# Side work of two feed-forward networks in another order, stores and copies issued by other engines, and a residual added one group later

## The chip, the cores and the metric

The kernel runs on one core of a Trainium2 chip, in one launch. The metric is the time in microseconds (us) of one execution on the device. Engines are named as in the profile: PE multiplies matrices (PEld loads its weights), DVE, ACT and POOL work on tiles, SP issues DMA transfers; sixteen DMA engines move the data.

## The reference, cut to what matters

One layer of a hybrid decoder for 1024 prompt tokens and 64 sample tokens (8 sequences of 8), with a model width of 1024:

```python
x = x + 0.5 * swiglu(rmsnorm(x, ffn1_norm), ffn1_w_gu, ffn1_w_down)
h = rmsnorm(x, mix_norm)
z = h @ w_in                                   # q, k, v, LRU inputs, memory queries, three gates
y_att = attend(q, k, v, rel_bias)              # dilated windows; new window caches are outputs
xc, conv_new = causal_conv(xr, conv_buf, conv_w, conv_b)
y_rec = gelu(yr) * rglru(xc, ...)
y_mem = memory_attention(qm, mk, mv)
merged = sum over branches of sigmoid(gate + b) * (y @ w_o)
x = x + merged @ w_out
x = x + 0.5 * swiglu(rmsnorm(x, ffn2_norm), ffn2_w_gu, ffn2_w_down)
y = rmsnorm(x, final_norm)
# swiglu(h, w_gu, w_down) = (silu(h @ gate) * (h @ up)) @ w_down, hidden width 2816
```

Each output window cache of the sample tokens is the old cache shifted by the 8 new rows, so most of it is a copy from memory to memory.

## The kernel before

All large products run as three matmuls with a high and a low part of both operands (`mac3`, L262 to L264). A weight tile `wr` of 512 columns is split by ACT into its high part (`part`, L167) and by DVE into the low part `ws` (L168). The plan of weights is fixed, SP loads the tiles in its order (L154), and seven split parts (`RING`) may be ready ahead. The stages follow each other: FFN1 gate and up (to 556 us), its down projection (to 815), memory branch, gates and attention (to 1396), the recurrent branch, called LRU (to 1745), the merge of the branches, the output projection (to 2000), FFN2 gate and up (to 2505), its down projection (to 2785), the last norm.

*FFN gate and up.* The 1088 tokens are two halves (`tp`) of 544, each in two chunks of 272 (`TC`). The hidden width has 22 tiles of 128. Three of them are plain (`plain`), with operands `xo` of the raw x split in high and low part; meanwhile the norms are made (`norms_of_blocks`: ACT squares, POOL adds in L412), x is multiplied by the gain vector (`gain_blocks`, L426 on POOL or L430 on ACT) and sums and differences of blocks of x are made (`sums_of_blocks`, L438). The other tiles are quads: seven products of sums of blocks instead of eight, in the order of `OPS`, which is 1, 6, 7, 5, 2, 4, 3. Their weights are sums and differences of quarters a11, a12, a21, a22 of the gate and up weights (`combined`, L183 on DVE and POOL). `swiglu` empties the banks: DVE writes `uu` and `sl` (L539, L554), POOL multiplies by 1/rms (L557, L561); then `gated_hidden` has ACT apply silu (L503), POOL multiply `sl` by `uu` (L506) and SP store the tile to memory as `h_d` (L509), two, three and four steps later. The last two quads of each half run for that half alone. At the start of each tile, `copies` issues cache copies on SP (L1539); there are 42 of them.

*Down projection.* `h_d` is loaded again and split; groups of two hidden tiles add to x in SBUF (`down_tile`, L645), 24 tiles of output per group. In FFN2 the x to add to is loaded from memory by SP before (L1790).

*LRU.* `lru_tile` runs six times; between its steps PE works on chunks of the gates (tile `z`, emptied by DVE in L1383), two gates per tile. `att_combine` joins the attention groups for eight blocks of 128 tokens as a side job (DVE's weights `mw`, POOL's L871 and L873, PE's transpose in L832). `merge` loads the branch outputs as `ystage` (L1414), has ACT and DVE split them (L1420, L1421) and multiplies.

*Order.* Every engine runs its instructions in the order in which the program emits them. `tick()` is called once in every product (after four of its k steps); it runs the functions that `later(n, f)` put down for n ticks on and one step of the generators in `K.first` and `K.side`. So a number of steps says how many products later something is emitted, not when it runs. Each DMA waits for an earlier one on the same one of eight lanes. `norm_chunk` makes 1/rms of a chunk: matmul with ones (L294), DVE (L296, L298), POOL's power (L299), a matmul that spreads it over the partitions (L306), and DVE's copy `rbc` (L307). The last norm scales by `final` (L1516, L1518).

## Time and profile before

| | us |
|---|---|
| median of 3 runs (2795.2 to 2798.28) | 2796.01 |
| the profiled execution | 2796.95 |
| its span, first to last instruction | 2795.1 |
| PE busy in it | 2673.1 (96%) |
| DVE, ACT, POOL busy | 1718.9, 892.1, 808.4 |
| mean granted clock of PE | 0.981 |

Busy times are of one execution. PE is busy when any matmul is in it, at full or at half clock; a granted clock below 1 in a stretch means that part of it ran at the lower level. A bracket behind a timeline row is the idle time of that engine before the row and what ended it.

### The profile page before, as it was taken

To read this page: it belongs to the slowest core of one execution; us is meant where nothing else is said; L and a number is where in the kernel's file an instruction comes from. 1 tells how busy PE (TensorE), PEld (TensorE's weight loads), DVE (VectorE), ACT (ScalarE), POOL (GpSimd) and SP (SyncE) were. 2 spreads that over 40 slices of the span, in tenths; PEclk is the share of its full clock that TensorE was granted. 3 is DMA by queue.
4 is the path that set the end of the run, shared out by engine and by line. 5 is a ranking of instruction groups with operands and counts; after the bars stand their busy time and mean duration, and the time that the engine had idled before them with its cause. 6 is when DMAs were issued, how large, how long until landed. Compare 5 with 4: busy or idle time off the path is not lost.

```text
span 2795.1 us, 46229 instructions
## 1 busy us (share of the span) xinstructions
PE 2673.1 (96%) x18076; PEld 2588.7 (93%) x18076; DVE 1718.9 (61%) x3003; ACT 892.1 (32%) x1693; POOL 808.4 (29%) x734
## 2 busy tenths in 40 slices
PE   7789999999999999999989999999989999989997
PEld 7789999899999899989978889899989999979997
DVE  5545666767774433567687556763556666666766
ACT  6222232311144322323334354421623232231112
POOL 4445554400030000112144211231445454440003
PEclk9899999999999999999999999999999999999998
DMA  4223434522234252565555432854526432243221
GB/s 163 82 101 136 157 127 135 208 89 94 94 139 142 75 163 79 175 194 178 172 157 157 142 100 73 281 175 164 180 96 220 167 109 79 77 138 120 89 77 64
DMA packets 180570, 374.97 MB, mean 134 GB/s; under 512 B 21288, under 2 KB 115688, under 8 KB 179680
## 3 DMA queue, kind: packets, MB, share of 16 engines
q1 hardware_dynamic: 180352, 372.02, 40.1%
q8 instruction: 142, 2.33, 0.3%
q14 instruction: 76, 0.62, 0.1%
HBM read 305.59 MB, written 113.16 MB: 150 GB/s over the span
## 4 chain that ended last, share of the span: by engine, by line
PE 79%; DVE 6%; POOL 4%; issue 4%; DMA 4%; ACT 2%; SPq 0%; DVEq 0%; ACTq 0%; POOLq 0%
PE pg L262 9%; PE pg L264 9%; PE pg L263 9%; PE z L262 7%; PE z L264 7%; PE z L263 7%; PE pd L262 6%; PE pd L263 6%; PE pd L264 6%; DMA h_d<-sl 2%; PE po L264 2%; PE po L263 2%; PE po L262 2%; PE o L811 1%; PE wo L262 1%
## 5 line engine op out<-in xcount | busy, mean ns | idle before, releaser
L262 PE MATMUL pg<-xo,ws 128*128 128x272 f32 x2512 | 735.6, 293 | 51.1 <-ACT ws L167 27.6
L264 PE MATMUL pg<-xo,ws 128*128 128x272 f32 x2512 | 730.7, 291 | 5.5 <-DVE ws L168 5.5
L263 PE MATMUL pg<-xo,ws 128*128 128x272 f32 x2512 | 730.4, 291 | 0.0
L167 ACT ACTIVATE ws<-wr 128x512 fp32r<-128x512 f32 x592 | 349.6, 614 | 979.2 <-PE pd L264 385.3
L168 DVE TENSOR_TENSOR ws<-wr,ws 128x512 fp32r<-128x512 f32 x592 | 482.3, 837 | 183.6 <-ACT ws L167 182.2
L262 PEld LDWEIGHTS pg<-xo,ws 128*128 128x128 f32 x2512 | 480.4, 191 | 57.0 <-ACT ws L167 28.0
L264 PEld LDWEIGHTS pg<-xo,ws 128*128 128x128 f32 x2512 | 480.1, 191 | 6.3 <-DVE ws L168 6.3
L263 PEld LDWEIGHTS pg<-xo,ws 128*128 128x128 f32 x2512 | 480.7, 191 | 0.0
L262 PE MATMUL z<-xg,ws 128*128 128x368 f32 (+1 forms) x1392 | 476.2, 342 | 1.1 <-DVE ta L1383 1.1
L264 PE MATMUL z<-xg,ws 128*128 128x368 f32 (+1 forms) x1392 | 458.2, 329 | 0.0
L263 PE MATMUL z<-xg,ws 128*128 128x368 f32 (+1 forms) x1392 | 457.9, 329 | 0.0
L645 DVE TENSOR_TENSOR x<-x,pd 128x352 f32<-128x352 f32 (+1 forms) x528 | 270.9, 530 | 153.0 <-PE pd L264 147.1
L262 PE MATMUL pd<-h,ws 128*128 128x368 f32 (+1 forms) x1056 | 348.8, 330 | 8.0 <-DVE x L645 8.0
L263 PE MATMUL pd<-h,ws 128*128 128x368 f32 (+1 forms) x1056 | 347.6, 329 | 0.0
L264 PE MATMUL pd<-h,ws 128*128 128x368 f32 (+1 forms) x1056 | 346.4, 328 | 0.0
L262 PEld LDWEIGHTS z<-xg,ws 128*128 128x128 f32 x1392 | 263.3, 189 | 16.4 <-issue 13.5
L263 PEld LDWEIGHTS z<-xg,ws 128*128 128x128 f32 x1392 | 263.7, 189 | 1.1
L264 PEld LDWEIGHTS z<-xg,ws 128*128 128x128 f32 x1392 | 262.6, 189 | 0.0
L262 PEld LDWEIGHTS pd<-h,ws 128*128 128x128 f32 x1056 | 199.4, 189 | 8.6 <-DVE x L645 8.6
L264 PEld LDWEIGHTS pd<-h,ws 128*128 128x128 f32 x1056 | 200.0, 189 | 0.0
L263 PEld LDWEIGHTS pd<-h,ws 128*128 128x128 f32 x1056 | 199.6, 189 | 0.0
L557 POOL TENSOR_TENSOR uu<-uu,rbc 128x544 f32<-128x544 f32 x76 | 109.3, 1442 | 290.3 <-DVE uu L539 290.0
(290 smaller groups left out, 3578.0 us busy)
## 6 DMA issues: line engine op xcount, KB each, us to landing
wr<-in_w_gu_dram SPq DMA_DIRECT2D x96, 512.0 KB
wr<-in_w_in_dram SPq DMA_DIRECT2D x58, 512.0 KB
qb<-qs_d SPq DMA_DIRECT2D x48, 512.0 KB
h_d<-sl SPq DMA_DIRECT2D x88, 272.0 KB
hr<-h_d SPq DMA_DIRECT2D x44, 544.0 KB
wr<-in_w_dn_dram SPq DMA_DIRECT2D x44, 512.0 KB
out_sk_dram<-in_cache_k_dram SPq DMA_DIRECT2D x16, 1020.0 KB
out_sv_dram<-in_cache_v_dram SPq DMA_DIRECT2D x16, 1020.0 KB
```

The costliest lines, as they stand in the source:

```text
L167: nc.scalar.activation(spl[:, 0, :n], src, AF.Copy)
L168: nc.vector.tensor_tensor(out=spl[:, 1, :n], in0=src, in1=spl[:, 0, :n].bitcast(F32), op=OP.subtract)
L262: nc.tensor.matmul(out, wh, xh, start=start and i == 0, stop=False, **more)
L263: nc.tensor.matmul(out, wh, xl, start=False, stop=False, **more)
L264: nc.tensor.matmul(out, wl, xh, start=False, stop=i == n - 1, **more)
L557: nc.gpsimd.tensor_tensor(out=t["uu"], in0=t["uu"], in1=rb, op=OP.mult)
L645: nc.vector.tensor_tensor(out=xa, in0=xa, in1=ps[:, :n], op=OP.add)
L811: nc.tensor.matmul(po[:, e], pt[:, h, j * 128:(j + 1) * 128], z["vt"][:, kb[j], e], start=j == 0, stop=j == len(kb) - 1)
```

## The change

- `combined` makes the two sums of weights first (`s1` and `s2` have tiles of their own, a22 is kept), issues POOL's subtraction into a21 before the first part and that into a12 before the part of a22.
- In `norms_of_blocks` the engine that adds the squares is an argument: DVE for one half, POOL for the other; each square is added by itself.
- In the plain phase of both FFNs the gains of both halves are issued step by step beside each other, one on ACT and one on POOL, and the sums of both halves are DVE's.
- `gated_hidden` runs silu, product and store 4, 5 and 7 steps later in quads and 1, 2 and 3 in plain tiles. The store is issued by ACT; the cache copies are issued by POOL.
- `lru_constants` is spread over 20 steps.
- `att_combine` lets two more steps pass for blocks 2 and 3; the first two LRU tiles have one gate fewer, and the two gates left over run in `merge`, one third ahead of the loads, one third behind them and one third between the splits.
- In FFN2's down projection the first group's tiles are copied by ACT into x; during the second group SP loads x row by row and POOL adds it, eight steps later.
- `norm_chunk` spreads its result two steps later in FFN1's down projection, and runs later at the end; DVE adds every second square of the last chunk; the finals come three steps later.

```diff
-            mix += [col("w_in", 18 + r), col("w_in", 24 + r)] + take(FILL[2])
+            mix += [col("w_in", 18 + r), col("w_in", 24 + r)] + take(FILL[2] - (r < 2))
...
-        s2 = self.sums.tile([128, 544], F32, name=self.uid("s2"), tag="s2", bufs=2)[:, :512]
+        s1, s2 = (self.sums.tile([128, 512], F32, name=self.uid("s2"), tag="s2", bufs=2) for _ in range(2))
...
+        tt(nc.vector, s1, a21, a22, OP.add)
+        tt(nc.vector, s2, s1, a11, OP.subtract)
+        tt(nc.gpsimd, a21, a11, a21, OP.subtract)
         put(1, a11)
         yield
-        put(4, a22)
-        tt(nc.vector, a22, a21, a22, OP.add)
-        tt(nc.vector, s2, a22, a11, OP.subtract)
-        tt(nc.gpsimd, a21, a11, a21, OP.subtract)
-        yield
         put(6, s2)
         yield
         put(7, a21)
         yield
-        put(5, a22)
+        put(5, s1)
         yield
         put(2, a12)
         tt(nc.gpsimd, a12, a12, s2, OP.subtract)
+        yield
+        put(4, a22)
         yield
         put(3, a12)
         yield
...
-    def norms_of_blocks(self, tp, xs, pool):
+    def norms_of_blocks(self, tp, xs, pool, eng):
...
+                for k in range(4):
                     if i or k:
-                        for e in range(2):
-                            nc.gpsimd.tensor_tensor(out=acc, in0=acc, in1=t[:, e], op=OP.add)
+                        t = self.sums.tile([128, 512], F32, name=self.uid("sq"), tag="s2", bufs=2)[:, :TC]
                     else:
-                        nc.gpsimd.tensor_tensor(out=acc, in0=t[:, 0], in1=t[:, 1], op=OP.add)
+                        t = acc
+                    nc.scalar.activation(t, self.block(xs, i, j)[:, k], AF.Square)
+                    if i or k:
+                        eng.tensor_tensor(out=acc, in0=acc, in1=t, op=OP.add)
...
-                        self.gated_hidden(p, tp, sl, uu)
+                        self.gated_hidden(p, tp, sl, uu, (1, 2, 3))
...
-    def gated_hidden(self, p, tp, sl, uu):
+    def gated_hidden(self, p, tp, sl, uu, steps=(4, 5, 7)):
...
-            nc.sync.dma_start(self.h_d[p, :, tp * TH:(tp + 1) * TH], sl.rearrange("p j n -> p (j n)"))
+            nc.scalar.dma_start(self.h_d[p, :, tp * TH:(tp + 1) * TH], sl.rearrange("p j n -> p (j n)"))
...
-        for n, f in ((2, silu), (3, mult), (4, store)):
+        for n, f in zip(steps, (silu, mult, store)):
...
-                        self.down_tile([wd(j, (o - o0) * 128) for j in range(nk)], ks, o, c)
+                        self.down_tile([wd(j, (o - o0) * 128) for j in range(nk)], ks, o, c, residual and g == 0)
+                    if residual and g == 1:
+                        residual(o)
...
-    def down_tile(self, ws, ks, o, c):
+    def down_tile(self, ws, ks, o, c, new=False):
         nc = self.nc
         t0, n = CH[c]
         ps = self.mm_bank("pd")
         self.mac3(ps[:, :n], [(w, tuple(self.h[k][:, s, t0:t0 + n] for s in range(2))) for w, k in zip(ws, ks)])
         xa = self.x[:, o, t0:t0 + n]
-        nc.vector.tensor_tensor(out=xa, in0=xa, in1=ps[:, :n], op=OP.add)
+        if new:
+            nc.scalar.activation(xa, ps[:, :n], AF.Copy)
+        else:
+            nc.vector.tensor_tensor(out=xa, in0=xa, in1=ps[:, :n], op=OP.add)
         self.tick()
...
-            for _ in range(3):
+            for _ in range(5 if b in (2, 3) else 3):
...
-        nc.vector.tensor_tensor(out=e, in0=lam, in1=neg, op=OP.min)
-        nc.scalar.activation(e, e, AF.Exp)
...
+
+        def low():
...
+        for n, f in ((6, low), (10, lambda: nc.scalar.activation(e, e, AF.Exp)), (14, inverse), (20, series)):
+            self.later(n, f)
...
-    def merge(self, pool, gates):
+    def merge(self, pool, last):
...
-        gates()
+        wg = [self.unit("w_in", 128) for _ in last]
+
+        def gates(c):
+            for f, w in zip(last, wg):
+                ps = self.mm_bank("z")
+                self.mac3(ps[:, :CH[c][1]], [(w(k, 0), self.xgk(c, k)) for k in range(KD)])
+                if c == 2:
+                    self.done()
+                self.gate_evac(f, c, ps)
+                self.tick()
+        gates(0)
         stage = self.xgp.tile([128, 2 * KD, CMAX], F32, name="ystage", tag="xg")
...
             load(2, k, 3 * j)
+        gates(1)
         for j, k in enumerate(TRI):
+            if j == 2:
+                gates(2)
             split(2, k, 3 * j)
...
-            self.tc.keep_in_program_order(self.nc.sync.dma_start(d, s))
+            self.tc.keep_in_program_order(self.nc.gpsimd.dma_start(d, s))
...
-    norms = [K.norms_of_blocks(tp, xs[tp], ev) for tp in range(2)]
+    norms = [K.norms_of_blocks(tp, xs[tp], ev, eng) for tp, eng in enumerate((nc.vector, nc.gpsimd))]
...
-        yield from K.gain_blocks(xs[0], g, nc.scalar)
+        for _ in zip(K.gain_blocks(xs[0], g, nc.scalar), K.gain_blocks(xs[1], g, nc.gpsimd)):
+            yield
         yield from K.sums_of_blocks(0, xs[0], nc.vector)
         spare.close()
         late.append(right(spare, "late1"))
-        yield from K.gain_blocks(xs[1], g, nc.gpsimd)
-        yield from K.sums_of_blocks(1, xs[1], nc.gpsimd, lambda: K.plained)
...
-                K.later(6 if c < 2 else 2, lambda: K.norm_chunk(c, acc[c], 3 if c < 2 else 2))
+                K.later(6 if c < 2 else 2, lambda: K.norm_chunk(c, acc[c], 5 if c < 2 else 2))
...
-                gate(FILL[2])
+                gate(FILL[2] - (i < 2))
...
-        K.merge(pool, lambda: gate(24))
+        K.merge(pool, gates)
...
-        yield from K.norms_of_blocks(0, xs[0], ev)
-        yield from K.gain_blocks(xs[1], g, nc.scalar)
+        yield from K.norms_of_blocks(0, xs[0], ev, nc.vector)
+        for _ in zip(K.gain_blocks(xs[1], g, nc.scalar), K.gain_blocks(xs[0], g, nc.gpsimd)):
+            yield
         yield from K.sums_of_blocks(1, xs[1], nc.vector)
...
-        yield from K.gain_blocks(xs[0], g, nc.gpsimd)
-        yield from K.sums_of_blocks(0, xs[0], nc.gpsimd, lambda: K.plained)
+        yield from K.sums_of_blocks(0, xs[0], nc.vector, lambda: K.plained)
...
-        K.first += [K.operands_of_blocks(1, xs[1], g, order, store(1)), K.norms_of_blocks(1, xs[1], ev)]
+        K.first += [K.operands_of_blocks(1, xs[1], g, order, store(1)), K.norms_of_blocks(1, xs[1], ev, nc.gpsimd)]
...
-        for o in range(KD):
-            nc.sync.dma_start(K.x[:, o], K.x_d[1][:, o])
...
+        def residual(o):
+            t = pool.tile([128, NT], F32, name=K.uid("xr"), tag="xr", bufs=2)
+            nc.sync.dma_start(t, K.x_d[1][:, o])
+            K.later(8, lambda: nc.gpsimd.tensor_tensor(out=K.x[:, o], in0=K.x[:, o], in1=t, op=OP.add))
...
-                K.sumsq(o, xa, acc[c], n)
+                K.sumsq(o, xa, acc[c], n, nc.vector if c == 2 and o % 2 else None)
...
-                K.later(3, lambda: K.norm_chunk(c, acc[c], 2))
+                K.later(5, lambda: K.norm_chunk(c, acc[c], 3))
                 for j in range(4):
-                    K.later(6 + j, lambda j=j: K.final(c, 2 * j))
...
+                    K.later(9 + j, lambda j=j: K.final(c, 2 * j))
...
+        K.down("w_dn2", ring, K.raw_tiles(pool), after2, residual)
```

First place: the end of the plain tiles of FFN1. These are POOL's rows before (`xs_108` is the x of the second half, `rs` the 1/rms, `sl` the hidden tile, `wr` a weight tile):

```order
L506 TENSOR_TENSOR sl_173<-sl_173,uu_174 128x544
L506 TENSOR_TENSOR sl_347<-sl_347,uu_348 128x544
L426 TENSOR_TENSOR xs_108<-xs_108,vec 128x4x272 x2
L506 TENSOR_TENSOR sl_558<-sl_558,uu_559 128x544
L426 TENSOR_TENSOR xs_108<-xs_108,vec 128x4x272 x2
L438 TENSOR_TENSOR xs_108<-xs_108 128x4x272 x4
L183 TENSOR_TENSOR wr_624<-wr_588,wr_624 128x512
L506 TENSOR_TENSOR sl_720<-sl_720,uu_721 128x544
```

and POOL's rows now, from the second gain row's place on:

```order
L425 TENSOR_TENSOR xs_108<-xs_108,vec 128x4x272
L505 TENSOR_TENSOR sl_173<-sl_173,uu_174 128x544
L425 TENSOR_TENSOR xs_108<-xs_108,vec 128x4x272
L299 TENSOR_TENSOR rs_572<-rs_572,mhalf 128x4
L425 TENSOR_TENSOR xs_108<-xs_108,vec 128x4x272
L1563 DMA out_sv_dram<-in_cache_v_dram 8x2x15360
L425 TENSOR_TENSOR xs_108<-xs_108,vec 128x4x272
L505 TENSOR_TENSOR sl_361<-sl_361,uu_362 128x544
L505 TENSOR_TENSOR sl_590<-sl_590,uu_591 128x544
```

DVE's rows now at the same place (`xo` are split operands, `pg` the banks of the plain tiles, `xs_107` is the first half):

```order
L374 TENSOR_TENSOR xo_4_93_730<-xs_107,xo_4_93_730 128x1088
L475 TENSOR_TENSOR sl_590<-pg_687,rbc 128x272
L475 TENSOR_TENSOR uu_591<-pg_716,rbc 128x272
L437 TENSOR_TENSOR xs_108<-xs_108 128x4x272 x3
L374 TENSOR_TENSOR xo_6_97_771<-xs_108,xo_6_97_771 128x1088
L374 TENSOR_TENSOR xo_7_99_800<-xs_108,xo_7_99_800 128x1088
L437 TENSOR_TENSOR xs_108<-xs_108 128x4x272
```

POOL's sums of `xs_108` in L438 are gone from its queue and stand in DVE's as L437, behind the evacuations of a plain tile; the gains stand further ahead, and a cache copy stands between two of them.

Second place: a quad of FFN1. SP's rows before, with the two stores of a quad and the copy behind them:

```order
L154 DMA wr_2872<-in_w_gu_dram 128x1024
L509 DMA h_d<-sl_2737 128x544
L509 DMA h_d<-sl_2751 128x544
L1539 DMA out_sk_dram<-in_cache_k_dram 16x16320
L154 DMA wr_3107<-in_w_gu_dram 128x1024
L154 DMA wr_3109<-in_w_gu_dram 128x1024
```

ACT's rows now (silu is L502, the weight parts L167, the stores L508):

```order
L167 ACTIVATE ws_2423<-wr_2150 128x512
L502 ACTIVATE sl_2292<-sl_2292 128x544
L502 ACTIVATE sl_2306<-sl_2306 128x544
L167 ACTIVATE ws_2461<-s_2419 128x512
L508 DMA h_d<-sl_2292 128x544
L167 ACTIVATE ws_2496<-wr_2152 128x512
L508 DMA h_d<-sl_2306 128x544
L167 ACTIVATE ws_2527<-s_2418 128x512
L167 ACTIVATE ws_2558<-wr_2150 128x512
```

and POOL's rows now in a quad:

```order
L556 TENSOR_TENSOR uu_1238<-uu_1238,rbc 128x544
L560 TENSOR_TENSOR sl_1286<-sl_1286,rbc 128x272
L560 TENSOR_TENSOR sl_1300<-sl_1300,rbc 128x272
L1563 DMA out_sk_dram<-in_cache_k_dram 2x8x16128
L183 TENSOR_TENSOR wr_1190<-wr_1188,wr_1190 128x512
L505 TENSOR_TENSOR sl_1286<-sl_1286,uu_1223 128x544
L505 TENSOR_TENSOR sl_1300<-sl_1300,uu_1238 128x544
```

The stores stand between weight parts of the next quad, one part apart; the copy stands behind the two L560 rows and ahead of the first weight difference and the products.

Third place: PE at the start of the LRU stage, the transposes of block 2 of `att_combine` (`oc`) among z chunks, before:

```order
L262 MATMUL z_14257<-xg_7987,ws_13991 128x352
L263 MATMUL z_14257<-xg_7987,ws_13991 128x352
L264 MATMUL z_14257<-xg_7987,ws_13991 128x352
L832 MATMUL t_14299<-ident,oc_13893 128x128 x2
L262 MATMUL z_14328<-xg_8093,ws_13865 128x368
L263 MATMUL z_14328<-xg_8093,ws_13865 128x368
```

and now (L1333 is the first matmul of the second LRU tile, on the output `xc` of its convolution):

```order
L262 MATMUL z_14435<-xg_8257,ws_14040 128x368
L263 MATMUL z_14435<-xg_8257,ws_14040 128x368
L264 MATMUL z_14435<-xg_8257,ws_14040 128x368
L1333 MATMUL g_14468<-xc_14307,lw_13881 128x352
L1333 MATMUL g_14471<-xc_14307,lw_13881 128x352
L836 MATMUL t_14474<-ident,oc_13942 128x128 x2
L262 MATMUL z_14507<-xg_8036,ws_14043 128x352
```

The transposes have moved behind two more z chunks, and two matmuls that need the convolution of LRU tile 1 now stand right before them.

## Rows read from the trace of the kernel before

**Rows 1.** The head of the page (the span; busy time, share of the span and count of each engine), and the core's mean granted TensorE clock.

```profile
span 2795.1 us, 46229 instructions
...
PE 2673.1 (96%) x18076; PEld 2588.7 (93%) x18076; DVE 1718.9 (61%) x3003; ACT 892.1 (32%) x1693; POOL 808.4 (29%) x734
...
core 0: 2795.1 us, clock 0.981
```

**Rows 2.** What PE waited for over the whole span: PE's output and line <- engine, output and line waited for: us in total, times, longest.

```profile
PE pg L262 <- ACT ws L167: 27.6, 3, 11.6
...
PE pd L262 <- DVE x L645: 8.0, 2, 7.0
PE t L832 <- POOL oc L873: 7.5, 1, 7.5
...
PE t L1003 <- ACT yt L834: 5.3, 1, 5.3
```

**Rows 3.** Eleven stretches: start and end in us, width, then busy time (and instructions) of PE, of its weight loads, of DVE, ACT and POOL, the granted TensorE clock, the busy share of the DMA engines, GB/s.

```profile
8.00:50.00 42.00, 32.88 (x220) 31.46 (x220) 22.45 (x51) 27.85 (x56) 24.81 (x31) 0.92 0.47 184
79.90:95.20 15.30, 0.94 (x4) 0.56 (x3) 5.15 (x6) 4.33 (x6) 11.31 (x5) 0.61 0.19 78
160.00:280.00 120.00, 107.47 (x806) 104.70 (x805) 62.84 (x111) 31.47 (x57) 62.67 (x68) 0.96 0.34 122
515.00:557.00 42.00, 35.44 (x242) 34.00 (x240) 30.86 (x49) 17.75 (x30) 19.36 (x14) 0.92 0.75 280
804.00:815.00 11.00, 8.30 (x42) 7.99 (x41) 10.88 (x22) 8.11 (x18) 8.85 (x8) 0.84 0.42 152
1396.00:1459.00 63.00, 49.10 (x264) 46.76 (x263) 55.38 (x88) 24.05 (x32) 28.57 (x28) 0.92 0.56 174
1748.00:1763.00 15.00, 8.71 (x37) 7.28 (x36) 6.27 (x7) 6.10 (x9) 0.00 (x0) 0.76 0.99 337
2056.00:2072.00 16.00, 5.27 (x28) 4.74 (x27) 7.63 (x9) 4.36 (x7) 10.11 (x5) 0.72 0.39 130
2464.00:2487.00 23.00, 17.84 (x123) 16.73 (x122) 17.65 (x28) 10.13 (x18) 10.42 (x7) 0.91 0.27 93
2505.00:2514.00 9.00, 2.03 (x8) 1.73 (x7) 3.15 (x6) 0.00 (x0) 0.45 (x1) 0.78 0.68 246
2766.00:2786.00 20.00, 12.26 (x68) 10.85 (x66) 15.82 (x32) 9.66 (x18) 12.01 (x11) 0.84 0.40 148
```

**Rows 4.** Timeline at the end of the plain tiles of FFN1, in the order of engines DVE, POOL, ACT, PE: start, duration, engine and line, operation, tiles, count, and in brackets the idle time before and what ended it.

```profile
57.60 3.94 DVE L438 TENSOR_TENSOR xs<-xs 128x1088 f32<-128x1088 f32 x3
...
75.90 0.42 DVE L476 TENSOR_TENSOR uu<-pg,rbc 128x272 f32<-128x272 f32 x1
...
77.37 3.96 POOL L426 TENSOR_TENSOR xs<-xs,vec 128x1088 f32<-128x1088 f32 x2
81.29 10.16 POOL L438 TENSOR_TENSOR xs<-xs 128x1088 f32<-128x1088 f32 x4
...
88.91 2.11 ACT L373 ACTIVATE xo<-xs 128x1088 fp32r<-128x1088 f32 x2 [12.93 <-POOL xs L438]
...
91.59 0.59 PE L262 MATMUL pg<-xo,ws 128*128 128x272 f32 x1 [11.62 <-ACT ws L167]
```

**Rows 5.** Around a late store, timelines of SP's DMA issues, of DVE and of PE, one step of the chain of waits (the store, from issue to landing), what DVE waited for between 95 and 300 us, and one stretch with the columns of rows 3. The last two are an issue and a use of a sl buffer in a later, undisturbed quad.

```profile
126.00 0.64 SPq L1539 DMA_DIRECT2D out_sk_dram<-in_cache_k_dram  x1
...
143.39 24.00 DMA h_d<-sl
...
167.48 0.44 DVE L554 TENSOR_TENSOR sl<-pg,rbc 128x272 f32<-128x272 f32 x1 [15.46 <-DMA h_d<-sl]
...
167.97 0.39 PE L262 MATMUL pg<-xo,ws 128*128 128x272 f32 x1 [4.40 <-DVE sl L554]
...
DVE sl L554 <- DMA h_d<-sl: 35.3, 4, 15.5
...
163.00:167.50 4.50, 0.57 (x5) 0.35 (x3) 0.02 (x1) 0.00 (x0) 0.00 (x0) 1.00 0.12 47
...
353.72 2.11 SPq L509 DMA_DIRECT2D h_d<-sl  x2
...
364.62 0.44 DVE L554 TENSOR_TENSOR sl<-pg,rbc 128x272 f32<-128x272 f32 x1 [1.05 <-PE pg L264]
```

**Rows 6.** The stretch around the two waits at the start of the LRU stage, with the columns of rows 3.

```profile
1436.00:1460.00 24.00, 11.23 (x46) 10.65 (x45) 20.85 (x47) 5.13 (x10) 11.56 (x13) 0.76 0.58 179
```

**Rows 7.** Timeline: ACT in the merge, DVE at the start of the second down projection, DVE near the end.

```profile
1757.43 3.15 ACT L1420 ACTIVATE ys<-ystage 128x1104 fp32r<-128x1104 f32 x3 [4.37 <-DMA ystage<-y_d]
...
2511.85 3.34 DVE L645 TENSOR_TENSOR x<-x,pd 128x352 f32<-128x352 f32 x7 [5.85 <-DMA x<-x_d]
...
2780.14 2.39 DVE L1516 SCALAR_TENSOR_TENSOR x<-x,vec,rbc 128x368 f32<-128x368 f32 x4
```

**Rows 8.** Timeline rows of POOL in two quads one after the other, the stretch between them with the columns of rows 3, and a row of ACT in the last, single quads.

```profile
337.04 1.80 POOL L183 TENSOR_TENSOR wr<-wr,wr 128x512 f32<-128x512 f32 x1 [3.92 <-DVE wr L183]
...
357.81 1.80 POOL L183 TENSOR_TENSOR wr<-wr,wr 128x512 f32<-128x512 f32 x1 [2.33 <-DVE wr L183]
...
337.00:357.80 20.80, 20.80 (x169) 20.80 (x168) 13.12 (x22) 6.09 (x11) 10.81 (x8) 1.00 0.58 173
...
541.63 0.63 ACT L167 ACTIVATE ws<-wr 128x512 fp32r<-128x512 f32 x1 [5.31 <-POOL wr L183]
```

More of the change, by code (lines that the diff above doesn't have):

```diff
@@ L405, in norms_of_blocks @@
             for i in range(2):
-                for k in (0, 2):
-                    t = self.sums.tile([128, 544], F32, name=self.uid("sq"), tag="s2", bufs=2)
-                    t = t.rearrange("p (k n) -> p k n", k=2)
-                    nc.scalar.activation(t, self.block(xs, i, j)[:, k:k + 2], AF.Square)
+                for k in range(4):
                     if i or k:
-                        for e in range(2):
-                            nc.gpsimd.tensor_tensor(out=acc, in0=acc, in1=t[:, e], op=OP.add)
-                    else:
-                        nc.gpsimd.tensor_tensor(out=acc, in0=t[:, 0], in1=t[:, 1], op=OP.add)
+                        t = self.sums.tile([128, 512], F32, name=self.uid("sq"), tag="s2", bufs=2)[:, :TC]
+                    else:
+                        t = acc
+                    nc.scalar.activation(t, self.block(xs, i, j)[:, k], AF.Square)
+                    if i or k:
+                        eng.tensor_tensor(out=acc, in0=acc, in1=t, op=OP.add)
                 if i:
@@ L460, in plain @@
             xo = self.xo[tp]
-            sl, uu = (pool.tile([128, 2, TC], F32, name=self.uid(x), tag=x, bufs=3) for x in ("sl", "uu"))
+            sl, uu = (pool.tile([128, 2, TC], F32, name=self.uid(x), tag=x, bufs=n) for x, n in (("sl", 3), ("uu", 3)))
             for j, ms in enumerate(((1, 2), (0, 3))):
@@ L614, in gate_up, with down @@
             self.tick()
-    def down(self, dn, pool, raws, after):
+    def down(self, dn, pool, raws, after, residual=None):
         for g, (k, nk, w) in enumerate(DOWN):
@@ L1255, in lru_constants, with inverse, series @@
         nc.gpsimd.tensor_scalar(neg, lam, -1.0, None, op0=OP.mult)
[L1256 to L1270 removed]
+        def low():
+            nc.vector.tensor_tensor(out=e, in0=lam, in1=neg, op=OP.min)
+            nc.vector.tensor_scalar(neg, neg, 0.0, 4.0, op0=OP.max, op1=OP.mult)
+        def inverse():
+            nc.vector.tensor_scalar(z, e, 2.0, None, op0=OP.add)
+            nc.vector.reciprocal(z, z)
+        def series():
+            nc.gpsimd.tensor_tensor(out=z, in0=z, in1=e, op=OP.mult)
+            nc.gpsimd.tensor_tensor(out=z2, in0=z, in1=z, op=OP.mult)
+            nc.gpsimd.memset(s, 1.0 / 21)
+            for d in range(19, 0, -2):
+                nc.gpsimd.tensor_tensor(out=s, in0=s, in1=z2, op=OP.mult)
+                nc.gpsimd.tensor_scalar(s, s, 1.0 / d, None, op0=OP.add)
+            nc.gpsimd.tensor_tensor(out=s, in0=s, in1=z, op=OP.mult)
+            nc.gpsimd.tensor_scalar(s, s, 8.0, None, op0=OP.mult)
+            nc.gpsimd.tensor_tensor(out=self.c4, in0=s, in1=neg, op=OP.add)
+            nc.gpsimd.tensor_scalar(self.cq, self.c4, -0.5, None, op0=OP.mult)
+        for n, f in ((6, low), (10, lambda: nc.scalar.activation(e, e, AF.Exp)), (14, inverse), (20, series)):
+            self.later(n, f)
     def lru_open(self, pool):
@@ L1604, in begin1 @@
         late.append(right(spare, "late1"))
-        yield from K.gain_blocks(xs[1], g, nc.gpsimd)
-        yield from K.sums_of_blocks(1, xs[1], nc.gpsimd, lambda: K.plained)
+        yield from K.sums_of_blocks(1, xs[1], nc.vector, lambda: K.plained)
     K.first.append(begin1())
@@ L1817, in after2 @@
             if o == KD - 1:
-                K.later(3, lambda: K.norm_chunk(c, acc[c], 2))
+                K.later(5, lambda: K.norm_chunk(c, acc[c], 3))
                 for j in range(4):
-                    K.later(6 + j, lambda j=j: K.final(c, 2 * j))
-        K.down("w_dn2", ring, K.raw_tiles(pool), after2)
+                    K.later(9 + j, lambda j=j: K.final(c, 2 * j))
+        K.down("w_dn2", ring, K.raw_tiles(pool), after2, residual)
     low2.close()
```

13 lines of the change are left out of this document (removed).

## Prediction

> **What bounds the kernel now.** I read the head of the page first [rows 1]: PE is busy for 2673.1 of 2795.1 us and its clock is 0.981 over the span, so at most 122 us of idle PE and some 2795.1 x 0.019 = 53 us of low clock could be had, and every other engine is far from full. The list of what PE waited for [rows 2] comes second: no wait is repeated hundreds of times; a few long ones stand out, weight parts above all (27.6 us in 3). Third, stretch by stretch, how much is lost where the diff touches [rows 3]. For each stretch I take width minus PE busy as idle, and (1 - clock) x width as the bound of what the low clock costs, because work at half clock takes twice as long:
> - start, 8 to 50: 9.1 idle, 3.4 clock
> - end of the plain tiles of FFN1, 79.9 to 95.2: 14.4 and 6.0, most of its little PE work being part of both
> - quads beside the long cache copies, 160 to 280: 12.5 and 4.8
> - last, single quads of FFN1 (515 to 557) and FFN2 (2464 to 2487): 6.6 and 3.4; 5.2 and 2.1
> - norm row at 804 to 815: 2.7 and 1.8
> - LRU start, 1436 to 1460 [rows 6]: 12.8 and 5.8
> - merge, 1748 to 1763: 6.3 and 3.6
> - plain end of FFN2, 2056 to 2072: 10.7 and 4.5
> - start of down2, 2505 to 2514: 7.0 and 2.0
> - tail, 2766 to 2786: 7.7 and 3.2
>
> These add to 95 idle and 41 clock: the change works where most of the loss is. PE's matmuls stay the same number, so nothing beyond this can be won.
>
> **The change part by part**, against the profiled execution (2796.95 us, span 2795.1), which is 0.9 us above the median.
>
> *Start and plain end of FFN1.* Today POOL does the gain of the second half (L426) and then its sums (L438): 3.96 us to 81.25, then 10.16 us for four sums, while ACT waits 12.93 us for them and PE 11.62 us [rows 4]. Afterwards DVE makes the sums, three of them right after its evacuations at about 75.9 [rows 4]; its own three for the first half took 3.94 us. The gain starts earlier, beside that of the first half, so it is no longer late: four at 2.0 to 2.5 us (3.96 for two, 10.16 for four, [rows 4]) from about 50, an estimate, end near 60. Three sums then end near 80, split and subtract (2.11 / 2 by ACT, and I take 1.3 for DVE) give a product at about 82.5 where PE began at 91.6: 9 us, and perhaps 4 of the 6 clock. At the start the norms of half 0 go from POOL to DVE (halving their chain), up to 5 of the 9.1 idle; against it the first cache copies now leave at once on POOL, beside the loads of inputs and weights, where SP today issues the first at 9.7: 0 to 5 us lost, I take 3. Sum -10, bounds -20 and -2.
>
> *Stores on ACT, copies on POOL.* One h_d store, issued at 143.39, landed 24.00 us later behind a copy issued at 126.00; DVE waited 15.46 us for its buffer, PE 4.40 us [rows 5]. Near the end of that wait DMA was 12% busy at 47 GB/s, two of sixteen engines: a copy of this form (2 x 8 x 16128, 1.03 MB in 16 pieces) uses two, takes about 1.03 MB / 47 GB/s = 22 us, and 22 / 8 = 2.7 us per piece. DVE had four such waits, 35.3 us together; PE's slack hides about 15.46 - 4.40 = 11 us of each. After the change a copy leaves once in a quad (20.8 us between two like rows of POOL, [rows 8]) and no backlog of two can stand before a store. A store leaves three of a quad's fourteen products later, 3 x 20.8 / 14 = 4.5 us; today the first one of a quad leaves at 353.72 and its buffer is written again at 364.62 [rows 5], so 6.4 of these 10.9 us are left. The copy leaves some 4 us ahead of it; if the store lands only when that copy does, 18 us on, DVE waits 18 - 6.4 = 11.6, about what PE's slack covers. Also lru_constants, a chain over POOL, DVE and ACT in this stretch, is spread over 20 steps. From 12.5 + 4.8 I take -8, bounds -17 and +5 (a store that is late by more in each of 8 quads). Moving issues off SP costs ACT 88 and POOL 42 of them, 0.64 us on SP each [rows 5]: ACT (busy 6.09 of 20.8 us in a quad) and POOL (10.81) [rows 8] are idle enough to hide these.
>
> *Plain end of FFN2.* The same edit, with no copies at a start: idle 10.7, clock 4.5; PE resumes after sums by DVE instead of 10 us of POOL. -8, bounds -13 and -2.
>
> *Single quads.* An ACT weight part waited 5.31 us for POOL's L183, which stood behind an L557 that waited for DVE [rows 8]. Now the subtraction into a12 is emitted before the part of a22, so it stands ahead of the next L557. Of 6.6 + 3.4 + 5.2 + 2.1 = 17.3 I take 5, since DVE (30.86 of 42 us) also waits and is waited for there; bounds -14 and 0.
>
> *Norm row at 806.* Its broadcast is issued two steps later and PE has other work in front: -4, bounds -4.5 and -2.
>
> *LRU start.* PE waits 7.5 us for L873 and 5.3 us for L834 [rows 2]. The transposes of block 2 and 3 move two z chunks back and the next tile's conv comes a gate earlier. DVE however is busy 55.38 of 63 us, and 20.85 of the 24 around the waits [rows 3, 6], and z chunks need DVE to empty their banks (L1383). So most of these waits become waits for L1383 or for the conv: -3, bounds -12 and +8.
>
> *Merge.* Six z chunks (gates 22 and 23) are now cut to lie between the y loads and splits; ACT's three splits waited 4.37 us for loads [rows 7]. A chunk is more than 3 us of PE work, so both gaps of 6.3 idle are covered, most of 3.6 clock with them: -7, bounds -10 and -4.
>
> *Start of down2.* The x loads that DVE waited 5.85 us for [rows 7] aren't needed by the first group any more: ACT copies, and x is added by POOL in the second group, 8 rows of 128x1088 at some 2.5 us (like L438, [rows 4]) beside 24 tiles. What is late next is the split of h. In FFN1 the same edge shows no long wait: of PE's two waits for L645, 8.0 us together, the longest was 7.0 [rows 2], so the other edge cost 1. -7, bounds -9 and -4.
>
> *Tail.* DVE's adds of the last chunk take over half of POOL's; but all eight finals of chunk 1 (4 took 2.39 us, [rows 7]) now stand directly before the last norm, 2.4 us more on the last chain, against part of the 7.7 us that PE idles there. +1, bounds -4 and +5.
>
> Sum: -10 - 8 - 8 - 5 - 4 - 3 - 7 - 7 + 1 = -51: 2796.95 - 51 = 2746.
>
> **The rivals.**
> *A. The queues don't part.* The trace shows one queue only, so whether a store on another passes a copy is open. If transfers on each of the sixteen engines only take turns, a store's pieces go one for one with the eight of the copy, 2.7 us each: 22 us instead of 24. Then the store term gives at most 3, and the start loses 5: 2746 + 5 + 2 = 2753, and up to 2765 if each of eight quads loses 1.5 us on a late weight load too. For it: only two engines were busy. Against: PE's 11 us of slack. The Trainium skill, "DMA: Bandwidth & Descriptors", section "Issuing engines are not separate DMA queues", says that DMAs of all issuers share the same engines and interleave, so that another issuer only saves issue time. The trace has no second issuer to test it with; by that rule the time would be this rival's.
>
> *B. The waits only move.* PE waits for DVE or ACT next at most edges, as DVE is 61% busy and more at each of them: half of the terms at plain ends, merge and down2 (32 / 2 = 16) and all of the single quads, LRU and store terms (16) stay: 2746 + 32 = 2778.
>
> *C. Slower: side engines blocked.* A copy that POOL issues holds POOL, or ACT stands at a store until POOL's product is done. POOL's own work in a quad is 10.81 of 20.8 us [rows 8]. FFN2 issues two copies in a quad; from (20.8 - 10.8) / 2 = 5 us each POOL is full, and at 10 us it ends 10 us late in each of some 11 quads: +110 less the other gains, 2797 + 110 - 43 = 2864. For it: nothing in the trace shows POOL issuing a DMA; SP's issue took 0.64 us. The lower bound of its price is 0.64, the upper one the 24 us of a landing; I take the row of the issue.
>
> **How the numbers follow.** Forecast 0.62, A 0.16, B 0.14, C 0.08. Less than 0.2% (5.6 us) is what a measurement of this kernel hardly tells from no change. Forecast and A are faster nearly always, B mostly: 0.62 + 0.155 + 0.095 = 0.87. Same: 0.05, from B. Slower: C's 0.08. The bounds of all terms together are -104 and +4; all ends don't meet on one side, so I take -88 to -13 of it: 2709 to 2784, which holds A and B and leaves C out.
>
> **What would show it.** In the changed profile: PE's wait for the first quad's weights at about 80 under 4 us; no DVE wait on an h_d store above 11 us; no PE wait at the two down edges above 2 us; POOL's rows in a quad not pushed by its DMA issues. Wrong if PE waits for POOL or for ws in each quad, if PE idle at 1396 to 1460 is as long as before, or if the first matmuls come later than today.

## The result and the profile after

| | us |
|---|---|
| after, median of 4 runs (2818.89 to 2826.52) | 2824.39 |
| before, beside them (2795.2 to 2799.76) | 2797.15 |
| after / before | 1.0094, 95% interval 1.0076 to 1.0111 |

The change made the kernel slower by 0.94%; 2746 (2709 to 2784) was forecast. The head of the page after, with its list of DMA queues (packets, MB, share of sixteen engines), and the mean clock, which answer to [rows 1]:

```profile
span 2822.5 us, 46271 instructions
...
PE 2680.3 (95%) x18076; PEld 2595.5 (92%) x18076; DVE 1755.2 (62%) x3018; ACT 910.8 (32%) x1747; POOL 808.7 (29%) x745
...
q1 hardware_dynamic: 166464, 303.85, 32.6%
q0 software_dynamic: 2272, 43.65, 4.3%
q10 hardware_dynamic: 12672, 24.52, 2.3%
...
core 0: 2822.5 us, clock 0.977
```

PE is busy 7 us longer for the same number of matmuls, at a mean clock of 0.977 for 0.981, and idle 20 us longer: that makes the 27 us. Stores (q10) and copies (q0) now have queues of their own. What PE waited for, to be read against [rows 2]:

```profile
PE pg L262 <- DVE sl L553: 27.6, 5, 8.5
PE pg L262 <- ACT ws L167: 22.6, 3, 11.6
PE pg L262 <- DVE uu L538: 15.7, 10, 3.1
...
PE pd L262 <- ACT x L647: 8.1, 1, 8.1
PE g L1333 <- issue: 7.5, 1, 7.5
PE t L678 <- DVE sl L553: 6.6, 1, 6.6
...
PE z L262 <- DVE ta L1394: 6.2, 2, 4.5
```

A new first line: 27.6 us for DVE's L553, the old L554, which writes `sl`, and 6.6 us more for the same line at L678. DVE in turn waited for the h_d stores, 87.2 us in place of 35.3 [rows 5]:

```profile
DVE sl L553 <- DMA h_d<-sl: 87.2, 7, 16.3
```

The balance by stage, in us, from the last matmul of each stage, DVE's rows L554 or L553 and its last row in the timelines of both profiled executions:

| stage | before | after | difference | forecast |
|---|---|---|---|---|
| start and plain tiles of FFN1, to the first `sl` of a quad | 132.1 | 127.2 | -4.9 | -10 |
| from there to the 17th `sl` | 187.7 | 224.9 | +37.2 | -8 |
| rest of FFN1 gate and up (its single quads) | 230.4 | 231.0 | +0.6 | part of -5 |
| first down projection | 267.9 | 265.0 | -2.9 | -4 |
| to the end of the merge's products | 1086.2 | 1088.7 | +2.5 | -10 |
| output projection | 98.8 | 100.6 | +1.8 | 0 |
| FFN2 to the last quad of both halves | 438.7 | 431.1 | -7.6 | -8 |
| its single quads | 57.8 | 55.8 | -2.0 | part of -5 |
| second down projection | 277.5 | 276.5 | -1.0 | -7 |
| last norm | 14.0 | 17.2 | +3.2 | +1 |

One stage holds more than the whole loss. In it each quad with a long copy goes like the first of the six here: rows of the timelines (POOL's issue of the copy, ACT's of two stores, DVE, PE) and the store's step in the chain of waits, from issue to landing:

```profile
134.89 0.62 POOL L1563 DMA_DIRECT2D out_sk_dram<-in_cache_k_dram  x1
...
143.02 0.33 ACTq L508 DMA_DIRECT2D h_d<-sl  x1
...
144.80 0.33 ACTq L508 DMA_DIRECT2D h_d<-sl  x1
...
143.02 16.14 DMA h_d<-sl
...
159.25 0.44 DVE L553 TENSOR_TENSOR sl<-pg,rbc 128x272 f32<-128x272 f32 x1 [12.29 <-DMA h_d<-sl]
...
159.75 0.39 PE L262 MATMUL pg<-xo,ws 128*128 128x272 f32 x1 [2.82 <-DVE sl L553]
```

The copy leaves 8.1 us ahead of the store, the store takes 16.14 us, DVE waits 12.29 us and PE 2.82; in the later quads DVE waits 12 to 16 us and PE up to 8.5. This stretch alone, with the columns of [rows 3]:

```profile
127.00:352.00 225.00, 181.74 (x1324) 177.44 (x1324) 129.91 (x175) 51.88 (x90) 100.97 (x100) 0.90 0.29 102
```

PE is idle for 43 us in 225, 34.2 of them in the waits for L553 above, and a clock of 0.90 means up to another 22 us. How the store and the copy share their two DMA engines shows in the trace's packet records: starts of 2,176-byte pieces of the two stores, count per half microsecond (stretches without any are left out).

```
143.5: 19   144.0: 83   144.5: 10   145.5: 58   146.0: 54
147.0: 1    148.0: 1    149.5: 1    150.5: 1    152.5: 1   153.0: 1   155.0: 1   155.5: 1
157.5: 4    158.0: 9    158.5: 8    159.0: 3
```

224 of 256 pieces pass in 3 us. The 32 left are the share of two of the sixteen engines (256 / 16 x 2): eight go one for each 64,512-byte piece of the copy, one every 2.5 us and engine, and the last 24 only when the copy has ended. So transfers on different queues take turns, which is rival A's mechanism. The rule of the Trainium skill ("DMA: Bandwidth & Descriptors", section "Queues, rings and completion order") that an engine goes round its queues agrees in kind with these starts; it gives some 9 to 17 descriptors as typical of a turn, here a turn was one piece.

The other places that the forecast spoke of: POOL's first copy, PE's first matmul, its first quad, its wait in the LRU stage; ACT in the second down projection; DVE at the end.

```profile
1.33 0.82 POOL L1563 DMA_DIRECT2D out_sk_dram<-in_cache_k_dram  x1 [0.90 <-POOLq L1940]
...
11.62 0.60 PE L262 MATMUL pg<-xo,ws 128*128 128x272 f32 x1 [11.62 <-ACT ws L167]
...
88.65 0.59 PE L262 MATMUL pg<-xo,ws 128*128 128x272 f32 x1 [7.49 <-ACT ws L167]
...
1498.40 2.10 PE L1333 MATMUL g<-xc,lw 128*128 128x352 f32 x3 [7.53 <-issue]
...
2538.00 2.30 ACT L647 ACTIVATE x<-pd 128x352 f32<-128x352 f32 x6 [6.16 <-DMA h_d<-sl]
...
2805.91 4.19 DVE L1540 SCALAR_TENSOR_TENSOR x<-x,vec,rbc 128x368 f32<-128x368 f32 x8
```

### The profile page after: what moved, and what is told of

Read it like the earlier page. It is cut to its first block, busy times and chain, and to the rows that moved or that the text cites. A ratio compares the mean times of both kernels' runs of the same rounds, so it can differ in the third digit from the quotient of the medians.

```text
span 2822.5 us, 46271 instructions
## 1 busy us (share of the span) xinstructions
PE 2680.3 (95%) x18076; PEld 2595.5 (92%) x18076; DVE 1755.2 (62%) x3018; ACT 910.8 (32%) x1747; POOL 808.7 (29%) x745
## 4 chain that ended last, share of the span: by engine, by line
PE 73%; DVE 8%; DMA 7%; POOL 5%; issue 3%; ACT 3%; SPq 0%; DVEq 0%; ACTq 0%; POOLq 0%
PE pg L262 7%; PE pg L264 7%; PE pg L263 7%; PE z L262 7%; PE z L263 6%; PE z L264 6%; PE pd L262 6%; PE pd L263 6%; PE pd L264 6%; DMA h_d<-sl 4%; DVE ws L168 2%; PE po L264 2%; PE po L263 2%; PE po L262 2%; PE o L815 1%
## 5 line engine op out<-in xcount | busy, mean ns | idle before, releaser
L262 PE MATMUL pg<-xo,ws 128*128 128x272 f32 x2512 | 738.3, 294 | 72.1 <-DVE sl L553 27.6
L167 ACT ACTIVATE ws<-wr 128x512 fp32r<-128x512 f32 (+1 forms) x550 | 325.4, 613 | 914.7 <-PE pd L264 357.6
L168 DVE TENSOR_TENSOR ws<-wr,ws 128x512 fp32r<-128x512 f32 (+1 forms) x550 | 465.0, 869 | 151.8 <-ACT ws L167 151.4
L649 DVE TENSOR_TENSOR x<-x,pd 128x368 f32<-128x368 f32 (+1 forms) x504 | 257.7, 529 | 134.4 <-PE pd L264 134.3
L262 PEld LDWEIGHTS z<-xg,ws 128*128 128x128 f32 x1392 | 264.3, 190 | 22.4 <-issue 13.1
L183 POOL TENSOR_TENSOR wr<-wr,s 128x512 f32<-128x512 f32 x42 | 56.8, 1353 | 377.4 <-DVE ws L168 377.4
```

The costliest lines, as they stand in the source:

```text
L167: nc.scalar.activation(spl[:, 0, :n], src, AF.Copy)
L168: nc.vector.tensor_tensor(out=spl[:, 1, :n], in0=src, in1=spl[:, 0, :n].bitcast(F32), op=OP.subtract)
L183: eng.tensor_tensor(out=out, in0=x, in1=y, op=op)
L262: nc.tensor.matmul(out, wh, xh, start=start and i == 0, stop=False, **more)
L649: nc.vector.tensor_tensor(out=xa, in0=xa, in1=ps[:, :n], op=OP.add)
```

## The experiments

All but one edit the changed kernel; the ratio is to the kernel before on the same chip. The theory at the start (T): the order of copy and store decides, since on two shared engines the store lands with the copy whatever the queue.

**Which part of the copies and stores costs 37 us.**

```diff
-  y.rearrange("b (q e) -> b q e", q=16 // nb)
+  y.rearrange("b (q e) -> q b e" if g == 1 else "b (q e) -> b q e", q=16 // nb)
```

> The changed kernel, with the eight copies of 2x8x16128 written in the order 8x2x16128, so that each spreads over eight DMA engines instead of two. Theory T (a store and a copy on other queues take turns piece for piece on the two DMA engines that the copy holds, so the store lands only with the copy; the copy now leaves about 8 us ahead of the stores instead of behind them): a copy then lasts about 6 us, the waits of DVE L553 for h_d (87 us in the changed kernel) fall below 10 us, the six long quads go back to 21 us, and the time falls from 2824 by 35 to 45 us, to 2779 to 2789. Rival P (the store is late because it is issued three products later, and by ACT): waits stay, 2818 to 2826. Rival Q (a copy through GpSimd's queue is slow whatever its form): a fall of less than 15 us, 2810 or more.

Measured: 2766.78 us, ratio 0.9886 (0.9869 to 0.9903). The copy in 8 x 2 pieces spreads over eight engines and landed 8 to 10 us after its issue; of DVE's wait 1.9 us are left, and PE has no idle time where it had 35 us in the changed kernel. The same stretch of `after` and of `shape8` (columns of [rows 3]), and DVE's wait in `shape8`:

```profile
130.00:310.00 180.00, 145.05 (x1055) 141.18 (x1055) 94.68 (x128) 40.14 (x69) 76.80 (x81) 0.91 0.27 95
```

```profile
130.00:310.00 180.00, 180.00 (x1427) 178.08 (x1426) 114.96 (x186) 56.26 (x98) 107.23 (x109) 1.00 0.39 137
```

```profile
DVE sl L553 <- DMA h_d<-sl: 1.9, 1, 1.9
```

The fall, 57.6 us, is over the 35 to 45 expected: the clean stretch takes 166.3 us, so even before the change 21 of its 187.7 were to be won, where I had taken 8. P and Q fall.

```diff
-            self.copies(copies)
+            self.later(9, lambda: self.copies(copies))
```

> The changed kernel, with each copy of a quad emitted nine products later, behind both stores of the quad before; queues and form as in the change. Theory T (order against the copy decides): the stores leave ahead of the copy and land in about 3 us, waits for h_d below 20 us, time 2780 to 2795. Rival P (step count and ACT's issue): 2818 to 2826. Rival Q (slow queue): the stores still meet the copy, 2805 or more.

The edit is in the quads. Measured: 2764.62 us, 0.9878 (0.9864 to 0.9893), below T's 2780 to 2795 as well. With form and queues of the change, and only the time of the copy against the stores moved back, the loss is gone. Waits of L553 for h_d: two, 11.1 us together. ACT issued the first store 1.7 us ahead of POOL's copy and the second beside it:

```profile
139.56 0.33 ACTq L508 DMA_DIRECT2D h_d<-sl  x1
...
141.33 0.33 ACTq L508 DMA_DIRECT2D h_d<-sl  x1
...
141.24 0.62 POOL L1563 DMA_DIRECT2D out_sk_dram<-in_cache_k_dram  x1
...
DVE sl L553 <- DMA h_d<-sl: 11.1, 2, 6.0
```

```diff
-    def gated_hidden(self, p, tp, sl, uu, steps=(4, 5, 7)):
+    def gated_hidden(self, p, tp, sl, uu, steps=(2, 3, 4)):
```

> The changed kernel, with silu, product and store 2, 3 and 4 products later in quads, as before the change. Theory T: the store leaves some 4 us sooner, still behind a copy that is only a few us old, and lands with it: waits for h_d still over 60 us, time 2810 to 2826. Rival P (the three later steps make the stores late): waits below 40 us, time 2785 to 2798.

Measured: 2823.89 us, 1.009 (1.0074 to 1.0107), 80.6 us of waits for h_d. The later steps aren't the cause: P falls here too.

The next three put the issue of copies, stores, or both back to SP, in the two lines of the diff that name the engine.

> The changed kernel, with the copies issued by SP again, stores by ACT. SP no longer passes the stores, so it reaches a copy with the weight loads of its quad, ahead of that quad's stores. Theory T (any queue takes turns, the order decides): waits for h_d stay between 40 and 100 us, time 2800 to 2826. Rival Q (GpSimd's software queue is at fault): waits as before the change, about 35 us, time 2785 to 2795.

Measured: 2768.71 us, 0.9896 (0.988 to 0.9913), 36.7 us of waits. The waits were as Q had them and the time was below Q's range, neither as I had worked T out; but copies_late excludes Q, as its copies go through GpSimd's queue. My error was where SP would stand: behind the weight loads, so that it issued the copy at 140.55, after ACT's stores at 135.11 and 136.88.

> The changed kernel with the stores issued by SP again (same steps), copies by POOL in the old form 2x8x16128. Theory T (the copy is ahead of the stores, whoever issues them, and on another queue it takes turns with them): waits for h_d of 60 to 110 us, time 2812 to 2840. Rival R (ACT's queue makes stores slow): waits under 40 us, time 2770 to 2795.

Measured: 2814.36 us, 1.0059 (1.0044 to 1.0074), 81.3 us of waits: T's range, R falls.

> The changed kernel with stores and copies both issued by SP, in the old form 2x8x16128; SP's order is then both stores, copy, weights, as before the change. Theory T (the order against the copy decides, not the queue): waits for h_d of 20 to 60 us as in the kernel before, time 2766 to 2782. Rival S (the later steps bring the stores behind the copies in any case): waits over 80 us, time 2805 to 2826.

Measured: 2768.68 us, 0.9898 (0.9884 to 0.9913), 54.1 us of waits; T's ranges, S falls. So the copies' move to POOL is what set them ahead of the stores: 2824 and 2814 us with it, 2769 and 2769 without, whoever issues the stores. DVE's waits for h_d in steps_early, copies_sp, stores_sp and both_sp:

```profile
DVE sl L553 <- DMA h_d<-sl: 80.6, 8, 14.9
...
DVE sl L553 <- DMA h_d<-sl: 36.7, 7, 18.7
...
DVE sl L553 <- DMA h_d<-sl: 81.3, 6, 14.7
...
DVE sl L553 <- DMA h_d<-sl: 54.1, 6, 13.9
```

The stretch of the quads isn't clean with copies on SP: it took 175.9 us in copies_sp and 184.5 in both_sp, the latter near the old kernel's 187.7. That both come near shape8's time is due in part to other stages: they reach the first `sl` of a quad at 123.4 and 122.1 us instead of 127.6, and both_sp's second down projection takes 270.6 instead of 276.4.

> The kernel before the change, with only the eight 2x8x16128 copies written as 8x2x16128. Theory T: its four waits of DVE L554 for h_d (35 us) fall under 5 us, and the stretch of the quads beside them loses most of its 12.5 us of idle PE and 4.8 of low clock: time 2780 to 2788. Rival Q (only copies of GpSimd's queue hurt): 2795 to 2799.

The kernel before, with the line of shape8. Measured: 2780.41 us, 0.994 (0.9923 to 0.9957). That is in T's range. No wait for h_d is left in its list, and the stretch of [rows 3] from 160 to 280, then 12.5 us idle at a clock of 0.96, has no idle time. From the first to the 17th `sl` it took 168.1 us, and in shape8, with the whole change, 166.3: with the copies spread, nothing else in the change costs time there. The stretch from 160 to 280:

```profile
160.00:280.00 120.00, 120.00 (x954) 119.04 (x953) 73.51 (x125) 37.65 (x67) 68.04 (x74) 1.00 0.41 140
```

**The smaller terms**, each on top of shape8 (2766.8).

```diff
-            mix += [col("w_in", 18 + r), col("w_in", 24 + r)] + take(FILL[2] - (r < 2))
+            mix += [col("w_in", 18 + r), col("w_in", 24 + r)] + take(FILL[2] - (r > 3))
...
-                gate(FILL[2] - (i < 2))
+                gate(FILL[2] - (i > 3))
```

> shape8 (2766.8), with the two gates that run in the merge taken from the last two LRU tiles instead of the first two. Theory D (the start of the LRU stage is short of DVE, and the change put the next tile's convolution a gate earlier there, so PE waits 7.6 us for it and 6.1 us for L1394): the convolution's wait goes, the stretch from the end of the first down projection to the end of the merge's products falls from 1090.2 to 1081 to 1086 us, time 2757 to 2763. Rival E (DVE is simply full there, waits only move on to L1394): stretch 1088 to 1091, time 2764 to 2769.

Measured: 2766.44 us, 0.9884 (0.987 to 0.9899); the stretch took 1087.8. The wait for the convolution is gone, and another, 6.57 us, stands in its place:

```profile
1441.16 0.66 PE L836 MATMUL t<-ident,oc 128*128 128x128 f32 x2 [6.57 <-DVE ss L1010]
```

E's range for the time, and between both for the stretch. Over the 17 profiled executions that stretch goes with who issues: with stores on ACT and copies on POOL it took 1087.4 to 1090.8 us (eight of them), in the other nine 1083.9 to 1087.5, whichever tiles the gates were taken from. What the gates in the merge are worth stays open, and no run shows why the issuers should matter there.

> shape8, with FFN2's down projection as before the change (x loaded ahead of it, DVE adds in every group). Theory F (both forms wait for the same thing: the memory of x becomes free only when the last h_d store has left it; the change moved the wait from the load to ACT's first copy, and its own xr loads slow that store): the wait comes back under DVE L649, 5 to 7 us, time 2766 to 2770. Rival G (the change's form is the better one, since the load isn't waited for): PE waits over 2 us more, time 2770 to 2775.

Without `residual`: x is loaded first, and DVE adds in every group. Measured: 2765.98 us, 0.9885 (0.9868 to 0.9901). The wait is DVE's again, as F had it, and G falls:

```profile
2483.35 0.66 PE L262 MATMUL pd<-h,ws 128*128 128x352 f32 x1 [7.32 <-DVE x L647]
```

> shape8, with the last norm as before the change (squares of the last chunk all on POOL, the earlier norm and finals). Theory H (eight finals ahead of the last norm lengthen the last chain): from the last down matmul to the end 14 us instead of 17.2, time 2762.5 to 2764.5. Rival I (the adds on DVE save what the finals cost): 2766 to 2769.

The last norm as before the change. Measured: 2767.17 us, 0.989 (0.9875 to 0.9905). The last chain took 14.0 us instead of 17.2 as H had it, but the second down projection 279.1 instead of 276.4: PE waits 3.70 us for POOL's sum there again. Both ways cost the same, and the time is I's.

> shape8, with the first cache copy emitted 14 products later. Theory J (the first copy, POOL's first instruction, delays the start-up loads): PE's first weight part comes at 7.8 to 8.2 us instead of 11.6, time 2762.5 to 2764. Rival K (another cause, for one the loads' own order): 11.6 stays, 2766 to 2768.

`self.later(14, ...)` around the first copy. Measured: 2766.98 us, 0.9891 (0.9877 to 0.9906). J holds for its place, PE starts at 8.24 us and not at 11.57; but the time is K's, since the first `sl` of a quad comes at the same 127.4. PE now waits 4.40 us for a weight part on which DVE spent 5.40 us, where the median of L168 is 0.69. The copies, issued at 48.44 and 55.52, did not hold up a weight load there: SP issued none between 17.3 and 58.8. POOL's rows ran beside this one of DVE's, but no run shows what stretched it.

```profile
8.24 0.60 PE L262 MATMUL pg<-xo,ws 128*128 128x272 f32 x1 [8.24 <-ACT ws L167]
...
53.39 5.40 DVE L168 TENSOR_TENSOR ws<-wr,ws 128x512 fp32r<-128x512 f32 x1 [4.59 <-ACT ws L167]
...
58.84 0.59 PE L264 MATMUL pg<-xo,ws 128*128 128x272 f32 x1 [4.40 <-DVE ws L168]
```

**The start of the second down projection.** In stores_sp and both_sp it took 270.9 and 270.6 us against 275 to 279 in the others, so the queue of the last store was tried there.

> shape8 (2766.8) with the h_d stores issued by SP, in the old place of SP's order. Theory M (with the stores on ACT, SP passes the last one and issues the hr and xr loads of the second down projection ahead of it, so it takes 7 us to land, and ACT's first copy into x waits for it; on SP it is issued first): PE's wait for L647 falls from 7.7 to about 3 us, the second down projection from 276.4 to 271 us, time 2759 to 2763. Rival N (the shorter wait seen in stores_sp and both_sp came with the old form of the copies): 276 us, time 2765 to 2768.

Measured: 2755.96 us, 0.9856 (0.9841 to 0.9871): 10.8 us under shape8, more than expected. In the profiles 5.7 us fall in the second down projection (270.7), 2.5 in the first (265.2) and 4.7 in the stretch up to the end of the merge's products, which was shorter in the other runs with stores on SP as well. SP's rows of shape8 and ACT's, and then SP's of s8_stsp:

```profile
2470.30 0.86 SPq L568 DMA_DIRECT2D hr<-h_d  x2
2471.25 0.92 SPq L1817 DMA_DIRECT2D xr<-x_d  x2
...
2473.96 0.33 ACTq L508 DMA_DIRECT2D h_d<-sl  x1
...
2480.69 2.30 ACT L647 ACTIVATE x<-pd 128x352 f32<-128x352 f32 x6 [5.65 <-DMA h_d<-sl]
...
2481.21 0.66 PE L262 MATMUL pd<-h,ws 128*128 128x352 f32 x1 [7.65 <-ACT x L647]
```

```profile
2466.05 0.33 SPq L508 DMA_DIRECT2D h_d<-sl  x1
2466.42 0.92 SPq L568 DMA_DIRECT2D hr<-h_d  x2
2467.44 0.85 SPq L1817 DMA_DIRECT2D xr<-x_d  x2
...
2468.85 0.43 PE L262 MATMUL pd<-h,ws 128*128 128x352 f32 x1 [2.92 <-ACT x L647]
```

In shape8 SP issues the loads `hr` and `xr` at 2470 to 2472 and ACT the last store at 2473.96; it keeps ACT's first copy waiting until 2480.69. In the packet records of shape8 the 128 pieces of that store start only from 2477.95 on, 4 us after the issue. In s8_stsp the store leaves first, its pieces start 0.8 us after the issue, and PE waits 2.92 us instead of 7.65. N falls, as this run has the new form of the copies.

> The same, with FFN2's down projection as before the change. Theory M: the wait is DVE's for x again, the down projection 276 to 278 us, time 2764 to 2769; so the later residual is worth its 5 to 7 us only with the stores on SP. Rival N (the residual edit gives nothing on either queue): the same time as s8_stsp within 2 us.

Measured: 2759.47 us, 0.987 (0.9854 to 0.9887): down projection 274.1, PE's wait for x 6.9. So the later residual is worth 3.4 us there with the stores on SP, and it was worth none with them on ACT. M was right in kind and too high; N's 2 us were passed, at 3.5.

**What the runs point to.**

> What the runs point to, in one kernel: the changed kernel with the copies in the form 8x2x16128 and issued by SP, and the two gates of the merge taken from the last LRU tiles. shape8 is 2766.8; copies on SP started PE 3.7 us sooner. Theory T with J: 2760 to 2765. If the start-up gain is given back at the plain end, as in s8_c0late: 2765 to 2768.

Measured: 2759.36 us, 0.9867 (0.9852 to 0.9881), 0.6 below the range of T with J. PE starts at 8.12 us and the first `sl` comes at 123.0, so with the copies on SP the gain at the start is kept.

> sp8_best (2759.4) with the stores on SP too: both queue moves undone, the copies in the form 8x2x16128, the merge's gates from the last LRU tiles. Theory M: 5 us less, 2752 to 2757. If SP's order makes the stores wait behind weight loads: waits for h_d over 20 us and 2758 or more.

Measured: 2750.64 us, 0.9839 (0.9824 to 0.9853); that is below M's range. The change with both of its queue moves undone, the copies spread over eight engines and the merge's gates taken from the last LRU tiles is faster than the kernel before by 1.6% and than the changed one by 2.6%.

## Why the prediction was wrong

The step that failed is *Stores on ACT, copies on POOL*: -8, bounds -17 and +5, measured +37.2. Its argument was that a copy per quad leaves no backlog, and that a store that lands with the copy makes DVE wait 11.6 us, which PE's slack covers. The wait was sized nearly right, 12 to 16 us; the slack was not. PE hid 7.5 to 11 us of each (14.05 - 6.57, 12.11 - 1.07), so that gaps of up to 8.5 us were left in the six quads, 34.2 us together, and the granted clock fell to 0.90 over the stretch. And the sum counted on fewer late stores, where there were more: before, SP issued both stores of a quad directly ahead of its copy, so only four late stores arose; on POOL the copy stood ahead of the stores in each of six quads, a backlog not of two copies but of one, each time. The order rows that I showed said so, the copy behind the two L560 rows and ahead of the products which the stores need; I priced the distance of 4 us (8.1 measured) and not what it replaced. Three of the signs that I had named for the forecast failed: PE's wait for the first quad's weights was 7.49 us and not under 4, DVE waited 16.3 us on a store and not 11, and PE 8.1 us at FFN2's down edge and not 2.

Rival A named the mechanism and had the sign of its effect wrong, at -3: it compared a store behind a copy before with a store beside one after. The rule of the Trainium skill that stood beside it ("DMA: Bandwidth & Descriptors", section "Issuing engines are not separate DMA queues"), that DMAs of all issuers run on the same engines and interleave, agrees with the 32 held pieces above. The rival's time, 2753 to 2765, did not come, as what counted was which transfer goes first. Rival C fell: POOL's row of an issue is 0.62 us, ACT's 0.33. Rival B, that the waits only move, held for four places: the single quads, the norm row, the start of the LRU stage and the start of down2.

The other terms. *Plain end of FFN2*: -7.6 for -8, right; PE's idle there fell from 10.7 to 3.5 us. *Start and plain end of FFN1*: -4.9 for -10; the first copy costs 3.7 us (11.62 against 7.84 in copies_sp) for the 3 taken, so the sums on DVE and the norms brought 8.6 of the 13 counted: PE's first quad starts at 88.65, where 82.5 was forecast plus that delay. *Single quads*: -1.4 for -5, PE still waits up to 3.1 us at a time for L538. *LRU start and merge*: +2.5 for -10. The merge came as forecast, its 6.3 us of idle fell to 0.5. At the LRU start the waits moved to L1394 (1.70 and 4.54 us) and to L1333, which reads the convolution (7.53, for which the profile names no releaser), as the text said. Part of what the merge gained was lost ahead of the LRU stage, in the wait of the next point. *Norm row*: -2.9 for -4 in the stage, which is within the 263.5 to 268.2 that it took in other runs. Its wait at L306 fell by 2 us, but PE waits 4.25 us instead at L294 for POOL's sums, 8 us behind the stage's last matmul and so in the next stage of the table. From POOL's first of these sums (809.19 and 842.73) to that row of PE it is 13.1 us before and 13.5 after: the wait moved, and the term was no gain. The rows: the merge after, against the stretch from 1748 to 1763 in [rows 3], and PE in the norms, two rows before and two after.

```profile
1787.70:1802.70 15.00, 14.52 (x86) 14.21 (x85) 11.59 (x17) 7.36 (x13) 1.82 (x2) 1.00 0.72 231
...
809.26 0.54 PE L306 MATMUL t<-ident,rs 128*128 128x128 f32 x3 [2.70 <-POOL rs L299]
...
822.32 0.80 PE L294 MATMUL t<-ones,acc 128*128 128x1 f32 x6
...
842.79 0.54 PE L306 MATMUL t<-ident,rs 128*128 128x128 f32 x3 [0.74 <-POOL rs L299]
...
856.27 0.80 PE L294 MATMUL t<-ones,acc 128*128 128x1 f32 x6 [4.25 <-POOL acc L321]
```

*Start of down2*: -1.0 for -7, because the change's own store on ACT was passed by SP's loads; s8_stsp shows -6.8. *Tail*: +3.2 for +1, in bounds.

sp8_all, without the failed step and without the store's side effect, took 2750.6, where 2746 was forecast for the change. That they are near is luck, as its gain lies elsewhere than I had it: in the profiles 19.7 us beside the copies (187.7 to 168.0) and 11.7 at the start (132.1 to 120.4).
